# A scratch tile's place, padded gate weights, a float32r mask and moved squares in a hybrid decoder kernel

## The chip, the core and the metric

The kernel runs on one core of one Trainium2 chip. The metric is the device time of one execution in microseconds (us). Engines are named as in the profile: PE is TensorE (matmuls), PEld its weight loads, DVE is VectorE, ACT is ScalarE, POOL is GpSimd, SP is SyncE, which issues the DMAs.

## What is computed

Two layers, one after the other, over 1024 tokens of width 1024 (all float32). A layer normalises its input, projects it, runs four token mixers side by side (stick-breaking attention, a state-space model called S5, retention, a gated linear recurrence called RG-LRU), gates them, and projects back:

```
def _layer(x, ...):
    h = _rms_norm(x, pre_g)
    proj = h @ w_in                                   # 1024 -> 7168
    y_sb  = stick_breaking_attention(q, k, v)         # 4 heads x 64, causal
    y_ssm = s5_branch(ssm_u, ...)                     # 16 groups, 64 complex states
    y_ret = retention(q, k, v)                        # 4 heads x 64
    y_lru = rg_lru_branch(lru_u, ...)                 # 4 blocks x 64, conv of width 4
    mix = stack(y_sb, y_ssm, y_ret, y_lru) * silu(gates)
    y = einsum("bsnw,nwd->bsnd", mix, w_branch)
    out = sum_n(sigmoid(merge_n) * y_n) @ w_out
    return x + _rms_norm(out, post_g)

def rg_lru_branch(u, conv_w, conv_b, w_a, b_a, w_x, b_x, lam):
    xb = conv(u).reshape(..., 4, 64)
    r  = sigmoid(einsum("bsnc,ncd->bsnd", xb, w_a) + b_a)     # gate weights: 64 x 64 blocks
    ig = sigmoid(einsum("bsnc,ncd->bsnd", xb, w_x) + b_x)
    a = exp(-8 * r * softplus(-lam))
    return scan(a, sqrt(1 - a*a) * ig * conv(u))
```

In the attention, a query sees only keys before it: the kernel adds -1e30 to the scores of the others (the causal mask). The S5 branch needs, once per layer, tables that depend on its parameters alone: powers of a complex decay, cosines and sines, products of them with the input and output matrices.

## The kernel before

**Units.** The work is cut into four units: layer 0 and layer 1, each in two chunks of 512 tokens. A unit walks through 64 weight tiles (`filler`): 16 tiles of projections for the mixers, four groups of 10 tiles (gate, merge gate and branch projection, one group for each mixer), and 8 tiles of the output projection. Each float32 product is made of three float32r products of a high and a low part (`mm3`: `hh*wh + hl*wh + hh*wl`), so a weight tile is split first: ACT copies the raw tile to `wh` (L86), DVE subtracts to get `wl` (L89). The splits run a tile and a half ahead of the matmuls; five buffers of `wh` and five of `wl` turn.

**Side tasks.** The mixers and the preparation of the next layer are generators (`first`, `prep`, `lru`, `s5`, `ret`, `sba`, `post`, `prologue`) that are stepped at places between the tiles; the table `PLAN` holds the places. The order of the instructions on each engine is the order in which this Python code issues them; nothing reorders them later. An engine does its instructions in that order, so one that waits holds up all behind it.

**Scratch tiles.** `G()` hands out one of 36 tiles of 128x512 (tag `g`), from a list of free ones. The first instruction that writes a tile waits for the last one that used the same place before.

**The S5 parameter task** (`prep`, L468) runs in unit 0 for layer 0 and in unit 1 for layer 1, nearly all of it on POOL, in some 230 small operations. Its tile `tmp = G()` (L471) is the scratch of the exponentials (`exp_head`, `exp_tail`) and then, as `t1`, of the loop that doubles the cosine and sine tables `tcos` and `tsin` (L432 is the helper `ptt`); the loop's last step, for columns 64 to 127, writes 128x512 in each operation. The DVE operations of `s5` read these tables.

**The gate weights** of RG-LRU (`lru_weights`) are the high part `wlh` (128 rows x 512) and the low part `wll` (256 columns; each block in the 64 rows of its half). In `lru`, for each of two column groups, PE does `wlh`, `wll`, `wlh`, `wll`, where the products with `wll` use 64 rows.

**The mask** (`sba`, for each of 4 token blocks x 4 heads in each unit): two float32r products of queries and keys, padded to at least 256 columns, then a bfloat16 product of the identity `identb` with the 128x128 triangle `trib` into the same bank.

**The first squares** (`first`, the start of unit 0): of eight tiles of the input, POOL squares the first four and sums them (L374, L376), ACT squares the other four, DVE adds those.

Of the kernel before, what the change touches and what calls it, by code (L numbers as in the profile page):

```python
# [9 lines left out]
F32 = mybir.dt.float32  # L10
F32R = mybir.dt.float32r
# [5 lines left out]
P = 128  # L17
# [26 lines left out]
def hybrid_kernel(ctx: ExitStack, tc: tile.TileContext, x, xt, ws1, ws2, par, bcw, preg, postg, con, rot, out, dbg=None):  # L44
# [6 lines left out]
    whp = ctx.enter_context(tc.tile_pool(name="whp", bufs=5))  # L51
    wlp = ctx.enter_context(tc.tile_pool(name="wlp", bufs=5))
    parp = ctx.enter_context(tc.tile_pool(name="parp", bufs=1))
    smp = ctx.enter_context(tc.tile_pool(name="smp", bufs=4))
    genp = ctx.enter_context(tc.tile_pool(name="genp", bufs=NGEN))
    psa = ctx.enter_context(tc.tile_pool(name="psa", bufs=3, space=bass.MemoryType.PSUM))
    psb = ctx.enter_context(tc.tile_pool(name="psb", bufs=5, space=bass.MemoryType.PSUM))
# [65 lines left out]
    xi = v3(cons[:, K_XI:K_XI + 256], P)  # L123
    zeta = cons[:, K_ZETA:K_ZETA + 4]
    cdec = cons[:, K_CD:K_CD + 2]
    identb = const.tile([P, P], BF16, name="identb")
    trib = const.tile([P, P], BF16, name="trib")
    kS = [const.tile([P, SEQ], F32R, name=f"kS{h}") for h in range(4)]
    vsb = const.tile([P, SEQ // P, 256], F32, name="vsb")
    uext = [const.tile([P, 3 + T], F32, name=f"uext{t}") for t in range(2)]  # L130
# [7 lines left out]
    tsin = const.tile([P, 8, P], F32, name="tsin")  # L138
    s5s = const.tile([P, 10, 8], F32, name="s5s")
    RHO, E1C, E1S, HCR, HCI, GCR, GCI = range(7)  # L140
    psc = const.tile([P, 16], F32, name="psc")
    rcar = const.tile([P, 2, 64], F32, name="rcar")
    wgh = const.tile([P, 512], F32R, name="wgh")
    wgl = const.tile([P, 512], F32R, name="wgl")
    wlh = const.tile([P, 512], F32R, name="wlh")
    wll = const.tile([P, 256], F32R, name="wll")
    sp8 = const.tile([P, 2], F32, name="sp8")
    x1 = dram.tile([SEQ, D], F32, name="x1")
    ubuf, ybuf = ([dram.tile([P, T], F32, name=f"{n}buf{h}") for h in range(2)] for n in "uy")
# [193 lines left out]
    def first():  # L343
        pr = S["par", 0] = parp.tile([P, NPAR], F32, tag="par", name=nm("par"))
        gc = pr[:, C_PG:C_PG + 8]
        act.preload_act_table_set(EXPSET)
        xk, xh, xl, sqs = [], [], [], []
        for k in range(KD):
            xk.append(G())
            sp.dma_start(xk[k], xt[k, :, 0:T])  # L350
            if k == 0:
                sp.dma_start(gc, par[0, :, C_PG:C_PG + 8])
                load_to(0)
            if k == 3:
                load_to(1)
        sp.dma_start(pr[:, 0:C_PG], par[0, :, 0:C_PG])
        sp.dma_start(cons[:, 0:P], con[:, 0:P])
        load_to(2)
        load_to(3)
        sp.dma_start(cons[:, P:], con[:, P:])  # L360
        lru_load(0)

        for k in range(KD):
            xh.append(G(F32R))
            xl.append(G(F32R))
            actv(xh[k], xk[k], AF.Identity, scale=gc[:, k:k + 1])
            stt(xl[k], xk[k], gc[:, k:k + 1], xh[k].bitcast(F32), ALU.mult, ALU.subtract)
            if k < 3:
                split_to(k)
            if k == 5:  # L370
                split_to(3)
            if k < 4:
                sqs.append(G())
                pool.tensor_tensor(sqs[k], xk[k], xk[k], op=ALU.mult)  # L374
                if k:
                    pool.tensor_tensor(sqs[0], sqs[0], sqs[k], op=ALU.add)  # L376
        S["h"] = (xh, xl)
        yield 0

        split_to(4)  # L380
        for k in range(4, KD):
            sqs.append(G())
            actv(sqs[k], xk[k], AF.Square)
        for k in range(4, KD):
            tt(sqs[0], sqs[0], sqs[k], ALU.add)
        yield 0
        yield 0
        yield 0
        yield 1
        y = token_rstd(sqs[0])  # L390
        yield 1
        rb = token_rows(y)
        evac_u(rb)
        hh = hp.tile([P, KD, T], F32R, tag="hh", name=nm("hh"))
        hl = hp.tile([P, KD, T], F32R, tag="hl", name=nm("hl"))
        for k in range(0, KD, 2):
            for j in (k, k + 1):
                stt(xk[j], xk[j], gc[:, j:j + 1], rb, ALU.mult, ALU.mult)
                copy(hh[:, j, :], xk[j])
            for j in (k, k + 1):  # L400
                tt(hl[:, j, :], xk[j], hh[:, j, :].bitcast(F32), ALU.subtract)
            yield 0
            if k == 2:
                set_h(hh, hl)
                for t in range(2):
                    dve.memset(uext[t][:, 0:3], 0.0)
                    tt(uext[t][:, 3:3 + T], S.pop(("lps", t)), rb, ALU.mult)
                    S["uext", t] = True
                    Bdone()
        lru_weights()  # L410
# [58 lines left out]
    def prep(l):  # L469
        pr = S["par", l]  # L470
        sc = G()  # L471
        tmp = G()

        def v(i):
            return sc[:, i * 8:(i + 1) * 8]
# [220 lines left out]
    def lru_weights():  # L696

        lw = S.pop("lw")
        w4 = wlh[:, :].rearrange("p (t h c) -> p t h c", t=2, h=2)
        for h in range(2):  # L700
            a, b = slice(64 * h, 64 * h + 64), slice(64 - 64 * h, 128 - 64 * h)
            z = v3(lw[a, 0:256], P)
            copy(w4[a, :, h, :], z)
            copy(w4[b, :, h, :], z)
            tt(v3(wll[a, :], P), z, w4[a, :, h, :].bitcast(F32), ALU.subtract)

    def lru(l, c):
        pr = S["par", l]
# [18 lines left out]
        for t in range(2):  # L727
# [3 lines left out]
            for h in range(2):  # L731
                n = 2 * t + h
                mm(ps[h], wlh[:, n * P:(n + 1) * P], xs[t][h], True, False)
                mm(ps[h], wll[half[h], t * P:(t + 1) * P], xs[t][h][half[h], :], False, True)
            rr[t], ii[t] = G(), G()
            for h in range(2):
                a, b = half[h], half[1 - h]
# [688 lines left out]

    with tc.manual_schedule():
        dve.memset(ones1, 1.0)
        warm = const.tile([P, T], BF16, name="warm")
        dve.memset(warm, 0.0)  # L1430
        ps = A()
        for _ in range(NWARM):
            mm(ps, warm[:, 0:P], warm)
        start("first", first())
        for t in (tmat, ore, oim):
            pool.memset(t, 0.0)
        for u, (l, c) in enumerate(units):
            for i in range(NTILE):
                if u == 0 and i == 8:
# [187 lines left out]
```

## Time and profile before

| | |
|---|---|
| median of 3 runs | 1888.51 us (1888.3 to 1888.53) |
| the profiled execution | 1889.16 us, span of its instructions 1887.4 us |
| mean granted clock of PE | 0.99 |
| busy: PE, DVE, ACT, POOL | 97%, 63%, 47%, 13% of the span |
| DMA | 193.95 MB, 103 GB/s on average |

How to read it: the span is cut by instruction records; "idle before" of an instruction is time in which its engine did nothing, and the name behind it is what ended that. A PE record is longer than the time that a matmul takes of a busy PE, since matmuls are pipelined; from start to start, two matmuls of 512 columns are 0.23 us apart. A granted clock of 1.00 is 2.4 GHz, 0.5 is 1.2 GHz; values between are stretches with both.

### The profile page before, as it was taken

To read this page: it belongs to the slowest core of one execution; us is meant where nothing else is said; L and a number is where in the kernel's file an instruction comes from. 1 tells how busy PE (TensorE), PEld (TensorE's weight loads), DVE (VectorE), ACT (ScalarE), POOL (GpSimd) and SP (SyncE) were. 2 spreads that over 40 slices of the span, in tenths; PEclk is the share of its full clock that TensorE was granted. 3 is DMA by queue.
4 is the path that set the end of the run, shared out by engine and by line. 5 is a ranking of instruction groups with operands and counts; after the bars stand their busy time and mean duration, and the time that the engine had idled before them with its cause. 6 is when DMAs were issued, how large, how long until landed. Compare 5 with 4: busy or idle time off the path is not lost.

```text
span 1887.4 us, 24840 instructions
## 1 busy us (share of the span) xinstructions
PE 1833.0 (97%) x9210; PEld 1501.4 (80%) x9210; DVE 1198.1 (63%) x2165; ACT 884.9 (47%) x1669; POOL 252.0 (13%) x579
## 2 busy tenths in 40 slices
PE   8979999999999999979999999999999999999997
PEld 6757888888878888858888788888888788888886
DVE  7767755455689576635548856655537895776454
ACT  5763444344475444525446634344354845344333
POOL 7872000020000002871200000000000000000001
PEclk9989999999999999989999999999999999999999
DMA  5231232324332222223344223242244322222233
GB/s 175 97 103 60 72 119 91 124 95 151 110 125 98 87 85 68 92 68 134 106 127 145 102 76 109 78 137 95 95 134 133 105 97 87 82 68 79 98 98 106
DMA packets 68856, 193.95 MB, mean 103 GB/s; under 512 B 9600, under 2 KB 18176, under 8 KB 68736
## 3 DMA queue, kind: packets, MB, share of 16 engines
q1 hardware_dynamic: 68736, 192.38, 30.4%
q8 instruction: 72, 1.18, 0.3%
q14 instruction: 48, 0.39, 0.1%
HBM read 179.11 MB, written 12.58 MB: 102 GB/s over the span
## 4 chain that ended last, share of the span: by engine, by line
PE 80%; POOL 8%; DVE 7%; ACT 3%; issue 2%; DMA 1%; SPq 0%; DVEq 0%; ACTq 0%; POOLq 0%
PE pa L101 63%; PE pb L101 15%; POOL g L432 4%; DVE g L89 2%; PE pb L1020 2%; DVE wl L89 1%; ACT g L86 1%; POOL psc L436 1%; DVE g L98 1%; POOL tcos L432 1%; DVE g L93 1%; POOL tsin L432 1%; POOL g L436 1%; ACT g L83 1%; DVE g L811 0%
## 5 line engine op out<-in xcount | busy, mean ns | idle before, releaser
L101 PE MATMUL pa<-hh,wh 128*128 128x512 f32 x1576 | 627.1, 398 | 13.3 <-ACT wh L86 13.3
L101 PE MATMUL pa<-hh,wl 128*128 128x512 f32 x1576 | 617.2, 392 | 17.7 <-DVE wl L89 17.6
L101 PE MATMUL pa<-hl,wh 128*128 128x512 f32 x1576 | 616.0, 391 | 0.0
L89 DVE TENSOR_TENSOR wl<-raw,wh 128x512 fp32r<-128x512 f32 (+1 forms) x512 | 373.5, 767 | 214.8 <-ACT wh L86 214.1
L89 DVE TENSOR_TENSOR g<-g,g 128x512 f32<-128x512 f32 (+7 forms) x432 | 295.8, 685 | 123.9 <-ACT g L86 104.7
L86 ACT ACTIVATE wh<-raw 128x512 fp32r<-128x512 f32 (+1 forms) x512 | 328.2, 686 | 90.0 <-PE pb L101 44.0
L101 PEld LDWEIGHTS pa<-hh,wl 128*128 128x128 f32 x1576 | 297.2, 189 | 83.8 <-DVE wl L89 20.6
L101 PEld LDWEIGHTS pa<-hh,wh 128*128 128x128 f32 x1576 | 297.9, 189 | 75.2 <-ACT wh L86 14.0
L101 PEld LDWEIGHTS pa<-hl,wh 128*128 128x128 f32 x1576 | 297.5, 189 | 58.3 <-DVE hl L89 0.2
L83 ACT ACTIVATE g<-pa 128x512 f32<-128x512 f32 x161 | 96.1, 597 | 497.0 <-PE pa L101 462.2
L89 DVE TENSOR_TENSOR g<-g,pa 128x512 f32<-128x512 f32 x128 | 87.5, 683 | 181.2 <-PE pa L101 164.8
L101 PE MATMUL pa<-g,wh 128*128 128x512 f32 x544 | 169.5, 391 | 4.5 <-DVE g L98 3.4
L86 ACT ACTIVATE g<-pb 128x512 f32<-128x512 f32 (+4 forms) x163 | 72.6, 472 | 143.7 <-PE pb L101 86.0
L906 POOL MEMSET g<- 128x512 f32 x8 | 4.0, 526 | 943.9 <-PE pb L101 943.9
L101 PEld LDWEIGHTS pa<-g,wh 128*128 128x128 f32 x544 | 102.2, 188 | 29.0 <-DVE g L98 5.0
L86 ACT ACTIVATE g<-g 128x512 fp32r<-128x512 f32 (+2 forms) x152 | 79.1, 521 | 71.4 <-DVE g L89 32.8
L101 PE MATMUL pa<-g,wl 128*128 128x512 f32 x272 | 106.0, 390 | 0.0
L83 ACT ACTIVATE g<-pb 128x512 f32<-128x512 f32 (+4 forms) x203 | 87.9, 514 | 23.8 <-PE pb L101 20.1
L86 ACT ACTIVATE g<-pa 64x128 fp32r<-64x128 f32 (+3 forms) x150 | 68.9, 459 | 47.3 <-PE pa L101 45.6
L101 PE MATMUL pa<-wh,g 128*128 128x512 f32 x256 | 79.6, 392 | 0.0
L101 PE MATMUL pb<-wh,g 128*128 128x512 f32 x256 | 79.2, 391 | 0.0
L89 DVE TENSOR_TENSOR g<-pa,g 128x512 f32<-128x512 f32 x51 | 35.7, 702 | 58.9 <-ACT g L83 34.8
(208 smaller groups left out, 2099.6 us busy)
## 6 DMA issues: line engine op xcount, KB each, us to landing
raw<-in_ws_dram SPq DMA_DIRECT2D x128, 640.0 KB, 3.9
raw<-in_ws_dram SPq DMA_DIRECT2D x127, 512.0 KB, 3.6
g<-x SPq DMA_DIRECT2D x32, 256.0 KB, 5.7
g<-in_xt_dram SPq DMA_DIRECT2D x16, 256.0 KB, 6.7
g<-in_x_dram SPq DMA_DIRECT2D x16, 256.0 KB, 3.1
x<-g SPq DMA_DIRECT2D x16, 256.0 KB, 2.1
out_dram<-g SPq DMA_DIRECT2D x16, 256.0 KB, 2.0
g<-in_rot_dram SPq DMA_DIRECT2D x8, 256.0 KB, 4.4
```

Source lines behind the costliest of these rows:

```text
L83: act.activation(out, in_, func, **kw)
L86: act.activation(out, in_, AF.Copy, **kw)
L89: dve.tensor_tensor(out, a, b, op=op)
L93: dve.tensor_scalar(out, a, s1, None, op0=op0)
L98: dve.scalar_tensor_tensor(out, in0=a, scalar=s, in1=b, op0=op0, op1=op1)
L101: pe.matmul(out, lhsT=lhsT, rhs=rhs, start=start, stop=stop)
L432: pool.tensor_tensor(out, a, b, op=op)
L436: pool.tensor_scalar(out, a, s1, None, op0=op0)
L906: pool.memset(t, 0.0)
L1020: pe.transpose(ps[:, q * P:(q + 1) * P], r[:, q * P:(q + 1) * P], ident)
```

## The change

Five edits. `prep` takes its scratch tile from the constant pool (`ptmp`), no longer from the 36 of `G()`. `wll` gets 512 columns and 128 rows like `wlh`, with zeros in the rows of the other half (a POOL memset at the start), and its products use all 128 rows. `identb` and `trib` are float32r. The first four squares go to ACT and their sums to DVE. The warm-up tile comes from `G()`, and the pool of small statistics tiles has three buffers, not four.

```
-    smp = ctx.enter_context(tc.tile_pool(name="smp", bufs=4))
+    smp = ctx.enter_context(tc.tile_pool(name="smp", bufs=3))
...
-    identb = const.tile([P, P], BF16, name="identb")
-    trib = const.tile([P, P], BF16, name="trib")
+    identb = const.tile([P, P], F32R, name="identb")
+    trib = const.tile([P, P], F32R, name="trib")
...
+    ptmp = const.tile([P, 512], F32, name="ptmp")
...
-    wll = const.tile([P, 256], F32R, name="wll")
+    wll = const.tile([P, 512], F32R, name="wll")
...
             if k < 4:
                 sqs.append(G())
-                pool.tensor_tensor(sqs[k], xk[k], xk[k], op=ALU.mult)
-                if k:
-                    pool.tensor_tensor(sqs[0], sqs[0], sqs[k], op=ALU.add)
+                actv(sqs[k], xk[k], AF.Square)
...
-        for k in range(4, KD):
+        for k in range(1, KD):
             tt(sqs[0], sqs[0], sqs[k], ALU.add)
...
     def prep(l):
         pr = S["par", l]
         sc = G()
-        tmp = G()
+        tmp = ptmp
...
-        w4 = wlh[:, :].rearrange("p (t h c) -> p t h c", t=2, h=2)
+        w4, l4 = (w[:, :].rearrange("p (t h c) -> p t h c", t=2, h=2) for w in (wlh, wll))
...
-            tt(v3(wll[a, :], P), z, w4[a, :, h, :].bitcast(F32), ALU.subtract)
+            tt(l4[a, :, h, :], z, w4[a, :, h, :].bitcast(F32), ALU.subtract)
...
                 mm(ps[h], wlh[:, n * P:(n + 1) * P], xs[t][h], True, False)
-                mm(ps[h], wll[half[h], t * P:(t + 1) * P], xs[t][h][half[h], :], False, True)
+                mm(ps[h], wll[:, n * P:(n + 1) * P], xs[t][h], False, True)
...
-        warm = const.tile([P, T], BF16, name="warm")
+        warm = G(BF16)
...
-        for t in (tmat, ore, oim):
-            pool.memset(t, 0.0)
+        for t in (tmat, ore, oim, wll):
+            pool.memset(t if t is not wll else t.bitcast(F32), 0.0)
```

The order of the instructions on PE and DVE stays, apart from those added and removed; what moves are the places of the `g` tiles, and with them the waits. In brackets stand the semaphores that an instruction waits for: `Pool_49` is POOL's count. On DVE in unit 0, at the rotary embedding of retention's keys, stood before (`pa` is a PE bank with a projection, `wl` the low part of a weight half-tile):

```order
L89 TENSOR_TENSOR wl_1198<-raw_1125,wh_1197 128x512 [waits DMAHW1_49,Activation_49]
L89 TENSOR_TENSOR g_1218<-pa_1178,g_1120 128x512 [waits PE_49,Activation_49,Pool_49]
L89 TENSOR_TENSOR g_1217<-g_1217,g_1121 128x512
L89 TENSOR_TENSOR g_1218<-g_1218,g_1217 128x512 [waits DVE_49]
L89 TENSOR_TENSOR wl_1255<-raw_1125,wh_1254 128x512 [waits Activation_49]
L89 TENSOR_TENSOR wl_1271<-raw_1179,wh_1270 128x512 [waits DMAHW2_49,Activation_49]
```

and now, with the same numbers one higher:

```order
L89 TENSOR_TENSOR wl_1199<-raw_1126,wh_1198 128x512 [waits DMAHW1_49,Activation_49]
L89 TENSOR_TENSOR g_1219<-pa_1179,g_1121 128x512 [waits PE_49,Activation_49]
L89 TENSOR_TENSOR g_1218<-g_1218,g_1122 128x512
L89 TENSOR_TENSOR g_1219<-g_1219,g_1218 128x512 [waits DVE_49]
L89 TENSOR_TENSOR wl_1256<-raw_1126,wh_1255 128x512 [waits Activation_49]
L89 TENSOR_TENSOR wl_1272<-raw_1180,wh_1271 128x512 [waits DMAHW2_49,Activation_49]
```

The product into `g_1218` (now `g_1219`) waits for POOL no longer: the count that it waited for was that of POOL's last write to `tsin`, which reads `tmp`, whose place `g_1218` had. On ACT in unit 1, in the second chunk's attention (`pb_7531` holds transposed weights of the attention), stood before:

```order
L83 ACTIVATE g_7527<-pa_7485 128x512 [waits PE_49]
L86 ACTIVATE g_7536<-pb_7531 128x512 [waits PE_49,Pool_49]
L86 ACTIVATE g_7543<-pb_7538 128x512 [waits DVE_49,PE_49]
L86 ACTIVATE wh_7615<-raw_7427 128x640 [waits Activation_49]
L86 ACTIVATE wh_7634<-raw_7486 128x512 [waits DMAHW0_49,DVE_49]
```

and now:

```order
L83 ACTIVATE g_7527<-pa_7485 128x512 [waits PE_49]
L86 ACTIVATE g_7536<-pb_7531 128x512 [waits PE_49]
L86 ACTIVATE g_7543<-pb_7538 128x512 [waits DVE_49,PE_49]
L86 ACTIVATE wh_7615<-raw_7427 128x640 [waits Activation_49]
L86 ACTIVATE wh_7634<-raw_7486 128x512 [waits DMAHW0_49,DVE_49]
```

The same wait for POOL's last `tsin` is gone there. New waits for POOL stand where DVE's part of S5 in unit 0 first reads the tables:

```order
L1057 SCALAR_TENSOR_TENSOR g_1510<-g_1510,ones_119 128x127
L89 TENSOR_TENSOR g_1511<-g_1511,g_1510 128x127 [waits DVE_49,PE_49]
L89 TENSOR_TENSOR g_1562<-pb_1552,tcos 128x512 [waits PE_49,Pool_49]
L89 TENSOR_TENSOR g_1564<-pb_1553,tsin 128x512 [waits PE_49,Pool_49]
L89 TENSOR_TENSOR g_1562<-g_1562,g_1564 128x512 [waits DVE_49]
```

Before, these two had no wait of their own for POOL, since DVE had waited for the same count earlier.

## Rows read from the trace of the kernel before

**Rows 1.** The page, engines: busy us, share of the span, instructions.

```profile
PE 1833.0 (97%) x9210; PEld 1501.4 (80%) x9210; DVE 1198.1 (63%) x2165; ACT 884.9 (47%) x1669; POOL 252.0 (13%) x579
```

**Rows 2.** The chain that ended last: start us, us, what (count).

```profile
248.44 13.68 PE pa L101 x60
```

**Rows 3.** Waits of PE, the longest: waiter, releaser, total us, times, longest.

```profile
PE pa L101 <- DVE wl L89: 17.8, 6, 10.4
PE pa L101 <- ACT wh L86: 13.8, 2, 13.3
```

**Rows 4.** Timeline of PE in unit 0: start us, us, instruction, idle before.

```profile
109.12 0.40 PE L101 MATMUL pa<-hl,wh 128*128 128x512 f32 x1
119.97 0.79 PE L101 MATMUL pa<-hh,wl 128*128 128x512 f32 x1 [10.44 <-DVE wl L89]
...
124.37 0.27 PE L1020 MATMUL pb<-cons,g 128*128 128x128 f32 x1
```

**Rows 5.** Timeline of DVE in unit 0.

```profile
98.17 1.48 DVE L89 TENSOR_TENSOR wl<-raw,wh 128x512 fp32r<-128x512 f32 x2
117.26 0.69 DVE L89 TENSOR_TENSOR g<-pa,g 128x512 f32<-128x512 f32 x1 [17.60 <-POOL tsin L432]
...
144.42 0.68 DVE L89 TENSOR_TENSOR g<-pb,tcos 128x512 f32<-128x512 f32 x1
```

**Rows 6.** Timeline of POOL, the last write of the table in units 0 and 1.

```profile
115.96 1.26 POOL L432 TENSOR_TENSOR tsin<-tsin,g 128x512 f32<-128x512 f32 x1
...
837.51 1.26 POOL L432 TENSOR_TENSOR tsin<-tsin,g 128x512 f32<-128x512 f32 x1
```

**Rows 7.** Stretches: length, busy us (count) of PE, PEld, DVE, ACT, POOL, clock, DMA.

```profile
120.00:124.40 4.40, 4.40 (x11) 3.35 (x12) 4.26 (x8) 0.00 (x0) 0.00 (x0) 0.51 0.68 209
...
840.50:844.60 4.10, 4.04 (x10) 3.01 (x11) 3.92 (x6) 2.05 (x5) 0.00 (x0) 0.51 0.52 155
```

**Rows 8.** Timeline of PE in unit 1.

```profile
826.84 0.39 PE L101 MATMUL pa<-hh,wl 128*128 128x512 f32 x1
840.56 0.79 PE L101 MATMUL pa<-hh,wh 128*128 128x512 f32 x1 [13.34 <-ACT wh L86]
...
844.57 0.63 PE L101 MATMUL pa<-g,wh 128*128 128x512 f32 x2
```

**Rows 9.** Timeline of ACT in unit 1.

```profile
838.80 1.08 ACT L86 ACTIVATE g<-pb 128x512 f32<-128x512 f32 x2 [23.40 <-POOL tsin L432]
```

**Rows 10.** Timeline of PE at RG-LRU's gates, unit 0, first of eight such places.

```profile
61.65 0.40 PE L101 MATMUL pb<-g,wlh 128*128 128x512 f32 x1
61.98 0.50 PE L101 MATMUL pb<-g,wll 64*128 64x512 f32 x1
...
63.60 0.40 PE L101 MATMUL pb<-hl,wh 128*128 128x512 f32 x1
```

**Rows 11.** Timeline of PE at a mask, unit 0, one of 64.

```profile
200.24 0.23 PE L101 MATMUL pb<-trib,identb 128*128 128x128 bf16 x1
...
200.59 0.40 PE L101 MATMUL pa<-hl,wh 128*128 128x512 f32 x1
```

**Rows 12.** Timeline of PE at plain float32 products of 128 columns.

```profile
231.37 0.39 PE L101 MATMUL pb<-g,ore 128*128 128x128 f32 x2
231.60 0.39 PE L101 MATMUL pb<-g,oim 128*128 128x128 f32 x2
```

**Rows 13.** Timeline of DVE, ACT and PE at the start.

```profile
5.82 0.69 DVE L89 TENSOR_TENSOR wl<-raw,wh 128x512 fp32r<-128x512 f32 x1 [0.41 <-ACT wh L86]
...
12.02 1.77 DVE L89 TENSOR_TENSOR wl<-raw,wh 128x512 fp32r<-128x512 f32 x1
13.72 3.89 DVE L98 SCALAR_TENSOR_TENSOR g<-g,par,g 128x512 fp32r<-128x512 f32 x3
...
15.33 2.18 ACT L83 ACTIVATE g<-g 128x512 f32<-128x512 f32 x4
...
15.29 0.50 PE L101 MATMUL pa<-g,wh 128*128 128x512 f32 x1 [1.48 <-DVE g L98]
```

## The prediction

> **What bounds the kernel now.** I read the page's engine shares first: PE is busy 97% of the span and POOL 13% [rows 1]. So a gain must come out of PE's time, and a slow engine matters only where PE waits for it. The chain of waits gives the price of a normal matmul: 60 of 512 columns in 13.68 us, 0.228 us each [rows 2]; this is the unit for everything below. Then PE's waits: the two lines that lead them, 17.8 and 13.8 us, hold one wait of 10.4 us behind DVE and one of 13.3 behind ACT [rows 3]. Both were followed back on the timelines.
>
> In unit 0, PE goes from a matmul at 109.12 straight to the next at 119.97 [rows 4]. It waits for a `wl`; DVE, which makes it, sat idle for 17.60 us until POOL's last `tsin` [rows 5], which ended at 115.96 + 1.26 = 117.22 [rows 6]. The instruction that DVE stood at is a rotary product that has nothing to do with the tables: by the order it writes a `g` tile on the place that `tmp` had, and `tmp` is read by that last `tsin`. In unit 1 the same happens on ACT: a copy of attention weights waits 23.40 us for `tsin` [rows 9], which ends at 838.77 [rows 6], the weight splits queue behind the copy, and PE stands from 826.84 to 840.56 [rows 8]. After each stop PE runs at a granted clock of 0.51, that is mostly 1.2 GHz, over the next 4 us [rows 7]. It had been idle just before both times.
>
> **The change part by part.** All against the profiled execution's 1889.16 us.
>
> 1. *The scratch tile.* The two waits for POOL are gone from the order, at the row that stalled in each case. First stop: 119.97 - 109.12 = 10.85 us where 0.23 is normal, so 10.62; then ten matmuls in 124.37 - 119.97 = 4.40 us where 2.28 is normal, so 2.12 for the low clock [rows 4]. Together 12.7. Second stop: 840.56 - 826.84 - 0.23 = 13.49, then nine matmuls in 844.57 - 840.56 = 4.01 against 2.05, so 1.96 [rows 8]. Together 15.4. Sum 28.2 (before rounding) us, all on PE's path. What is late next? DVE gets its idle 17.60 us back and then leads PE by more than before, since PE's own stop was shorter by 7 us. The tables are first needed at 144.42, by DVE [rows 5]; with 13 to 15 us taken away before it, that read comes at about 130, and POOL is done at 117.22 even if it gains nothing. So the new wait for POOL there finds its count reached.
>
> 2. *Full-row `wll`.* From the first `wlh` at 61.65 to the second ordinary matmul after the group at 63.60 there are five intervals, 1.95 us where five normal ones are 1.14 [rows 10]. The 0.81 us is lost wherever 64-row and 128-row products follow each other. There are eight such places (4 units x 2 column groups, 16 products with `wll`): 6.5 us. With 128 rows the form is that of any other float32r product, so I take all of it; the other end is nothing. The memset of `wll` and the strided write of its halves lie on POOL and DVE with nobody waiting. The Trainium skill, "TensorE: Matmul & The Clock Gate", section "Why this matters for your kernels", speaks against this edit: a product with few rows takes the time of a full one, and its gain is that it can run beside others. By that rule padding buys nothing and this term is 0, so the sum would be 6.5 us smaller. The row disagrees here, with 0.39 us for an interval where the rule has 0.23, so I go by the row.
>
> 3. *The float32r mask.* Before, from the mask to the second matmul behind it is 200.59 - 200.24 = 0.35 us: mask plus one full product [rows 11]. No float32r product under 256 columns is in the trace, so the price is bounded by the float32 ones of 128 columns: two records in 0.23 us, 0.115 each [rows 12]. If float32r does it in one such pass, the group takes 0.115 + 0.228 = 0.343: 64 masks gain 0.5 us. If it needs two, as each plain float32 product does, it takes 0.23 + 0.228, 0.108 more than now: 64 masks lose 6.9. I take one pass, since all wider float32r products run as one record each.
>
> 4. *The first squares.* POOL's squares run beside DVE and both slow: the same `wl` takes 0.69 us alone and 1.77 beside a square, and three of the low parts of the input take 3.89, 1.30 each; PE stops for the fourth at 15.29 [rows 13]. Without POOL's squares DVE wins 1.08 + 0.61 = 1.7 there and more before it, while the squares that ACT now does (0.55 each, four in 2.18 us) stand partly before the high parts. I take a gain of 1.5 us. Ends: the two waits of this kind, 3.0 gained, and all four squares on the path, 2.2 lost. The three extra adds on DVE, 0.7 each, come in its queue before the fifth and later weight splits; they lie beside matmuls of the first tiles, and if they did not, they would be 2 us.
>
> 5. *The rest at nothing.* POOL starts the S5 task some us earlier, which after edit 1 nobody waits for; if that cover were gone, it would be a gain. The warm-up tile in `G()` is free long before its place is taken again. The small tiles that lose a buffer are written and read by DVE in its own order in the attention, so a third buffer is enough.
>
> Sum: 28.2 + 6.5 + 0.5 + 1.5 = 36.7. 1889.16 - 36.7 = 1852.5; the profiled execution lies 0.65 above the median of the runs, so 1851.8 for a median.
>
> **The rivals.** *The mask needs two passes*: 7.4 us worse than assumed, 1859.2. For it: the code pads the query products to 256 columns, as if fewer were dear. Against: the wider ones show no sign of a second pass. 18%.
>
> *Half rows are not the cause* of the 0.81 us at the gates (the change of operands could be): 1858.3. This is what the page's rule above would make of it. Against: the neighbours with 128 rows follow each other at 0.23, with changing operands. 4%.
>
> *One of the two stops only moves*: another `g` tile lands on a place that POOL, or an engine behind it, holds long, or DVE's queue is too full in the stretch that is now denser. That gives back 12.7 or 15.4: 1864.5 or 1867.2. For it: DVE is close to full after the first stop, 4.26 of 4.40 us [rows 7]. Against: the order shows POOL's count at no other instruction near the two. 11%.
>
> *The change does not free the place*: the tile is freed, but the first writer there waits for POOL by another tile. That is 28.2 back, 1880.0. Against: the order's rows. 1%.
>
> *Slower than before.* Only the mask is repeated often enough: 64 times on PE. It would have to eat the other 36.2 us, 0.57 us more for each mask than now, over twice a full 512-column product, for instance if its weights could not be loaded beside the product before. The mixed forms at the gates cost 0.16 more for a product (0.39 against 0.23) [rows 10]. It decides from 0.57 us on: at 0.63, 64 x 0.63 = 40.3 against 36.2, 1892.6. 3%.
>
> **How the numbers follow.** 63% for the forecast's own case. The forecast is 1851.8. The range: below, squares at their better end and some us of small waits at the start and in unit 0, 1846; above, the mask's two passes (1859.2) with the squares at their worse end (3.7 more), or the first stop moved (1864.5), 1865. About 0.2%, 3.8 us, can be told from no change by measurement. Every case but the last is faster by more than that: the nearest to 1888.5 is the place that is not freed, 8.5 us below. So faster 0.95, slower 0.03, and 0.02 for within 0.2%, taken off the faster cases (a mask somewhat dearer than two passes, or errors that add up).
>
> **What would show it.** In the profile after: no wait of DVE or ACT for `tsin` over 1 us, no gap of PE over 6 us, and granted clock 1.00 where the two stops were; `wll` with 128 rows and 0.23 us from start to start; the mask as 64 records (128 would be two passes), with some 0.34 us to the second matmul behind it; the first `wl` splits at 0.7 us and PE's tile 1 done 1 to 2 us earlier. Wrong would be: PE's stops back at other places under another name, a mask that takes over 0.4 us, or POOL's tables still on the chain.

## The result, and the profile after

The changed kernel takes 1861.72 us (median of 4 runs, 1861.34 to 1862.88), the kernel before 1888.52 (4 runs, 1888.3 to 1888.82). The ratio is 0.986 with a 95% interval of 0.9842 to 0.9876: 26.8 us faster where 36.7 were forecast. The time lies in the stated range, but a quarter of the gain is missing. The profiled execution took 1862.88 us, its span is 1861.1.

The page's engine line, to be laid beside [rows 1]:

```profile
PE 1826.2 (98%) x9210; PEld 1508.6 (81%) x9210; DVE 1200.8 (65%) x2168; ACT 888.2 (48%) x1673; POOL 258.1 (14%) x573
```

PE is still the bound, and its busy time shrank by 6.8 us (1833.0 to 1826.2): 19.5 of the 26.3 us by which the span is shorter are waiting that went. Its longest waits are no longer those of [rows 3]:

```profile
PE pa L101 <- DVE wl L89: 13.5, 8, 4.2
...
PE pa L101 <- ACT wh L86: 0.5, 1, 0.5
```

Of the 13.8 us behind ACT 0.5 are left. Behind DVE the longest is now 4.2 (a stop in unit 2 that was 4.69 before), but there are eight waits where there were six. Two of the new ones stand in unit 0, where the first stop was [rows 4]:

```profile
111.18 0.27 PE L1019 MATMUL pb<-cons,g 128*128 128x128 f32 x1
...
117.91 0.50 PE L101 MATMUL pa<-hh,wl 128*128 128x512 f32 x1 [2.91 <-DVE wl L89]
...
126.04 0.50 PE L101 MATMUL pa<-hh,wl 128*128 128x512 f32 x1 [2.39 <-DVE wl L89]
```

The row at 111.18 is the one that stood at 124.37: PE reaches it 13.2 us earlier, as forecast. Then it stands twice, for a low part each time. The reader should now look at DVE in that stretch, against [rows 5]:

```profile
108.05 1.30 DVE L89 TENSOR_TENSOR wl<-raw,wh 128x512 fp32r<-128x512 f32 x2 [4.54 <-ACT wh L86]
...
113.44 0.69 DVE L89 TENSOR_TENSOR g<-pa,g 128x512 f32<-128x512 f32 x1
114.05 2.36 DVE L89 TENSOR_TENSOR g<-g,g 128x512 f32<-128x512 f32 x2
116.33 2.98 DVE L89 TENSOR_TENSOR wl<-raw,wh 128x512 fp32r<-128x512 f32 x2
119.23 0.68 DVE L89 TENSOR_TENSOR g<-pa,g 128x512 f32<-128x512 f32 x1
...
124.49 2.43 DVE L89 TENSOR_TENSOR wl<-raw,wh 128x512 fp32r<-128x512 f32 x2
```

and at POOL beside it, against [rows 6]:

```profile
110.80 1.45 POOL L431 TENSOR_TENSOR tcos<-tcos,g 128x512 f32<-128x512 f32 x1
112.21 1.95 POOL L431 TENSOR_TENSOR ptmp<-tsin,g 128x512 f32<-128x512 f32 x1
...
118.84 1.63 POOL L431 TENSOR_TENSOR tsin<-tsin,ptmp 128x512 f32<-128x512 f32 x1
```

No wait for `tsin` is left. But POOL's last table step, which before ran from 110.50 while DVE stood still for it, now runs beside DVE's work, and both are slower: POOL's six operations take 1.45 to 1.95 us where they had 1.04 to 1.26, and two low parts take 2.98 us at 116.33 against 1.30 at 108.05.

One wait of DVE for POOL is left in this stretch, and it stood there before too, outside the rows of the prediction. First the kernel before, then the changed one:

```profile
148.58 0.69 DVE L89 TENSOR_TENSOR g<-pb,tcos 128x512 f32<-128x512 f32 x1 [1.33 <-POOL g L432]
```

```profile
142.24 0.69 DVE L89 TENSOR_TENSOR g<-pb,tcos 128x512 f32<-128x512 f32 x1 [1.67 <-POOL g L431]
```

It is not for the tables. In the program of either kernel this product writes a `g` tile on the place that `sc` had, the other scratch tile of `prep` (one line above `tmp`), and waits for the last POOL product that reads `sc`. It is the same kind of wait as the one that edit 1 takes away; experiment 4 comes back to it.

How much PE is ahead of the kernel before, at the same matmul of both traces:

| matmul (start before, after) | ahead | what lies between |
|---|---|---|
| 22.36, 19.88 | 2.47 | the opening |
| 29.91, 29.16 | 0.75 | low clock in after |
| 80.09, 77.77 | 2.32 | gates of unit 0, two places |
| 94.16, 93.41 | 0.75 | two waits for low parts |
| 124.37, 111.18 | 13.19 | the first stop is gone |
| 136.88, 130.70 | 6.18 | the two new stops |
| 175.95, 171.32 | 4.63 | low clock behind a stop of 1.85 |
| 826.84, 820.32 | 6.51 | gates of unit 1, masks |
| 844.57, 822.59 | 21.98 | the second stop is gone |
| 1799.95, 1773.67 | 26.28 | gates of units 2 and 3, the stop in unit 2, masks |

The places of low clock, by stretches (columns as in [rows 7]; the clock is the last but two):

```profile
24.00:28.00 4.00, 4.00 (x12) 3.30 (x12) 3.33 (x16) 0.00 (x0) 3.06 (x12) 0.59 0.79 259
...
127.00:131.00 4.00, 4.00 (x16) 2.59 (x16) 3.93 (x7) 1.63 (x4) 3.92 (x7) 0.57 0.85 311
168.00:172.00 4.00, 4.00 (x19) 3.71 (x18) 1.52 (x3) 2.12 (x4) 0.84 (x2) 0.57 0.00 0
```

In each of them PE is busy throughout, much of the time at the lower level of 1.2 GHz. None of the three stretches was low in the kernel before.

The other edits, first the gates (columns as in [rows 10]):

```profile
60.94 0.39 PE L101 MATMUL pb<-g,wlh 128*128 128x512 f32 x1
61.17 0.39 PE L101 MATMUL pb<-g,wll 128*128 128x512 f32 x1
61.40 0.39 PE L101 MATMUL pb<-g,wlh 128*128 128x512 f32 x1
61.63 0.40 PE L101 MATMUL pb<-g,wll 128*128 128x512 f32 x1
61.87 0.39 PE L101 MATMUL pb<-hh,wh 128*128 128x512 f32 x1
```

0.23 us from start to start, as wanted. Then a mask, against [rows 11]:

```profile
195.72 0.22 PE L101 MATMUL pb<-trib,identb 128*128 128x128 f32 x1
195.78 0.44 PE L101 MATMUL pa<-hh,wh 128*128 128x512 f32 x1
196.06 0.40 PE L101 MATMUL pa<-hl,wh 128*128 128x512 f32 x1
```

One record for each mask and 0.34 to the second matmul behind it: one pass.

### The profile page after: what moved, and what is told of

Same layout as the page of the kernel before. It is cut to its first block, busy times and chain, and to the rows that moved or that the text cites. A ratio compares the mean times of both kernels' runs of the same rounds, so it can differ in the third digit from the quotient of the medians.

```text
span 1861.1 us, 24840 instructions
## 1 busy us (share of the span) xinstructions
PE 1826.2 (98%) x9210; PEld 1508.6 (81%) x9210; DVE 1200.8 (65%) x2168; ACT 888.2 (48%) x1673; POOL 258.1 (14%) x573
## 4 chain that ended last, share of the span: by engine, by line
PE 85%; DVE 8%; ACT 5%; issue 1%; DMA 1%; SPq 0%; DVEq 0%; ACTq 0%
PE pa L101 66%; PE pb L101 16%; DVE g L89 2%; PE pb L1019 2%; ACT g L86 2%; ACT g L83 1%; DVE wl L89 1%; DVE g L98 1%; DVE g L93 1%; ACT wh L86 1%; DMA raw<-in_ws_dram 1%; DVE g L810 0%; PE pb L254 0%; ACT kS L86 0%; DVE g L1057 0%
## 5 line engine op out<-in xcount | busy, mean ns | idle before, releaser
L83 ACT ACTIVATE g<-g 128x512 f32<-128x512 f32 (+2 forms) x98 | 57.1, 602 | 31.1 <-DVE g L89 22.8
```

Of the source, the lines that this page charges most:

```text
L83: act.activation(out, in_, func, **kw)
```

## The experiments

Twelve runs follow; the ratios are against the kernel before, measured beside them (medians 1888.07, 1889.25 and 1887.95). Times of four executions of one kernel spread over 1 us and more, so beside the times one measure of the trace is used throughout: how long PE takes from the last matmul before the first stop (109.12 in before) to a matmul behind the stretch (170.52 in before). It is 61.40 us in before, and would be 61.40 - 12.7 = 48.7 with the first stop taken out. In after it is 164.32 - 108.40 = 55.92. The missing 7.2 us are what most of the experiments are about.

**1. The scratch tile alone** (`b_ptmp`, on the kernel before):

```
+    ptmp = const.tile([P, 512], F32, name="ptmp")
...
-        tmp = G()
+        tmp = ptmp
```

> The kernel before with edit 1 alone: the scratch tile has its own place. Theory A (after the first stop DVE is the bound of its stretch, and its late work meets POOL's last table step): of the first stop only some 5 to 6 us stay won at PE, the second stop is won whole (15.5), so 1888.5 - 21 = 1867.5, within 1.5, with PE standing again for 2 to 3 us each at the next two low parts of the weights. Rival B (the sum of the prediction: both stops lie whole on PE's path): 1888.5 - 28.2 = 1860.3, and what the changed kernel lacks against 1851.8 comes from another edit.

Measured: 1869.13 us (1866.45 to 1871.75), ratio 0.9897 (0.988 to 0.9913). PE's measure is 56.66, nearly that of after. In the trace the second stop gives back 15.5, the first 6.65 at first, of which 2.06 go by 151 (1.5 of it at a stop that experiment 4 explains) and 3.10 by 174, the latter mostly at low clock. So rival B falls: the edit by itself does not bring 28.2, and what is missing does not come from another edit. Theory A is right on the second stop and too kind on the first: 1.5 stay there by 174, where it had 5 to 6. The new stop:

```profile
118.82 0.80 PE L101 MATMUL pa<-hh,wl 128*128 128x512 f32 x1 [3.14 <-DVE wl L89]
```

**2. The full-row gate weights alone** (`b_wll`, on the kernel before): the wider `wll`, its memset, and

```
-                mm(ps[h], wll[half[h], t * P:(t + 1) * P], xs[t][h][half[h], :], False, True)
+                mm(ps[h], wll[:, n * P:(n + 1) * P], xs[t][h], False, True)
```

> The kernel before with edit 2 alone: full-row gate weights. Theory A (in this kernel the first stop ends at a time that POOL sets, so what PE wins before it in unit 0 is waited away): six of the eight places count, 6 x 0.81 = 4.9, so 1883.6. Rival B (all eight count): 6.5, so 1882.0. By the page's rule that few rows take the time of a full product and padding wins nothing: 1888.5.

Measured: 1885.99 us (1885.18 to 1888.13, 10 runs), ratio 0.999 (0.998 to 0.9999). In the trace each of the eight places gives its 0.80, 6.4 in all, so the edit does what the row promised. By the rule of the Trainium skill that the prediction names nothing would be won; the trace does not bear that out. But only 3.3 reach the end. In unit 0 PE is 1.55 ahead at 85.95, 0.62 at 87.10 and no longer at 94.21; the rest went in two stretches where the low clock lasted longer (0.65 behind the second stop, 1.01 in unit 2). Where the 1.6 go, PE shows:

```profile
87.10 0.50 PE L101 MATMUL pa<-hh,wl 128*128 128x512 f32 x1 [0.77 <-DVE wl L89]
94.21 0.51 PE L101 MATMUL pa<-hh,wl 128*128 128x512 f32 x1 [1.38 <-DVE wl L89]
```

and DVE, with the low parts in question:

```profile
86.36 1.30 DVE L89 TENSOR_TENSOR wl<-raw,wh 128x512 fp32r<-128x512 f32 x2
...
93.36 1.45 DVE L89 TENSOR_TENSOR wl<-raw,wh 128x512 fp32r<-128x512 f32 x2
```

In the kernel before the same low parts start at 86.41 and 93.42, 0.05 later: DVE did not move, though PE came 1.6 earlier. Theory A had the loss in the right unit and at the wrong place: not the first stop swallows it, but these two short waits ahead of it.

**3. The last table step left out** (`a_nolast`, on the changed kernel). It leaves out the last doubling of layer 0's cosine and sine tables, columns 64 to 127, and fills them with constants:

```
+            if l == 0 and j == 6:
+                pool.memset(tcos[:, :, hi], 1.0)
+                pool.memset(tsin[:, :, hi], 0.0)
+            else:
                 ptt(tcos[:, :, hi], tcos[:, :, lo], cb, ALU.mult)
...
```

> The changed kernel, but in layer 0 the last step of the table's doubling (six POOL operations of 128x512) is left out and two POOL memsets fill the columns. Theory A1 (PE's two new stops, 2.91 and 2.39 us, come from DVE being slowed by POOL's table step beside it): DVE's low parts near 116 go from 1.49 to about 0.65 each, the first stop falls to about 0.8 us, the second to nothing, and the low clock after it goes: 1861.7 - 4.5 to 6 = 1856 to 1857. Rival A2 (DVE has simply too much in its queue there, POOL or not): the stops stay within 1 us of 2.91 and 2.39, and the time within 1.5 of 1861.7.

Measured: 1858.52 us (1855.37 to 1859.92), ratio 0.9842 (0.9827 to 0.9857). PE's measure falls from 55.92 to 51.78. The stops:

```profile
115.29 0.50 PE L101 MATMUL pa<-hh,wl 128*128 128x512 f32 x1 [0.91 <-DVE wl L89]
...
122.48 0.50 PE L101 MATMUL pa<-hh,wl 128*128 128x512 f32 x1 [1.46 <-DVE wl L89]
```

2.4 us in place of 5.3, and no low clock between 100 and 160. The first stop came out as A1 said; the second stayed at 1.46 where A1 had nothing. That does not show a queue of DVE that is too full without POOL, for POOL is at work there too:

```profile
117.68 1.82 DVE L98 SCALAR_TENSOR_TENSOR g<-g,g 128x512 f32<-128x512 f32 x1
117.65 1.31 POOL L431 TENSOR_TENSOR wgl<-g,wgh 128x512 fp32r<-128x512 f32 x1 [3.52 <-ACT wgh L86]
```

The same DVE operation takes 0.69 in after, at 121.67, so 1.13 of the 1.46 may be this one meeting. Of the missing 7.2 us the table step is 4.1.

**4. The table step done twice** (`a_twice`, on the changed kernel), the opposite of 3:

```
+            for _ in range(2 if l == 0 and j == 6 else 1):
+                ptt(tcos[:, :, hi], tcos[:, :, lo], cb, ALU.mult)
...
```

> The changed kernel with the last step of layer 0's table doubling done twice (the same six POOL operations of 128x512 again, with the same result). Theory A1 (POOL's wide operations slow DVE beside them): the second round runs from 120 to about 130, DVE's operations there take half as long again or more, and PE's second stop grows from 2.39 to 4 or more. Rival A2: the stops near 115 and 124 stay within 0.7 of 2.91 and 2.39. Under both, DVE's wait for POOL near 142 grows from 1.67 to 8 to 11, so the whole time is 1867 to 1873 either way; the stops decide, not the time.

Measured: 1868.59 us (1867.3 to 1871.45), ratio 0.9895 (0.988 to 0.991). PE's measure rises to 60.83, by 4.9. The stops:

```profile
120.77 0.79 PE L101 MATMUL pa<-hh,wl 128*128 128x512 f32 x1 [5.42 <-DVE wl L89]
...
130.56 0.50 PE L101 MATMUL pa<-hh,wl 128*128 128x512 f32 x1 [2.38 <-DVE wl L89]
```

It was the first stop that grew, not the second, and DVE's later wait for POOL grew only to 3.03, not to 8 or more; both expectations were off there. The amount speaks plainly: a table step less takes 4.1 us off PE's time in this stretch, one more puts 4.9 on. In DVE's own time, from the start of the two low parts at 108.05 to the end of those at 124.49, the same 22 operations without a gap in each trace:

| | us |
|---|---|
| before (119.23 to 134.48; POOL idle for 10.86 of it) | 15.25 |
| `a_nolast` (107.07 to 123.37) | 16.30 |
| after (108.05 to 126.92) | 18.87 |
| `a_twice` (108.37 to 131.25) | 22.88 |

Both runs change a second thing, the end of POOL's work, and with it the wait for the place of `sc`: DVE's product with `tcos` that waits there starts at 136.91 in `a_nolast` and at 142.24 in after. Here are it and PE's stop that follows, in `a_twice`:

```profile
148.12 0.69 DVE L89 TENSOR_TENSOR g<-pb,tcos 128x512 f32<-128x512 f32 x1 [3.03 <-POOL g L431]
154.87 1.15 PE L101 MATMUL pb<-g,g 128*64 128x64 f32 x32 [0.64 <-DVE g L89]
```

In six traces (`a_twice`, `b_ptmp`, `a_bf16`, `a_poolsq`, `a_half2`, `after_again`) PE stands at this matmul, for 0.64 to 1.45 us, and each time starts it 6.75 or 6.76 us after that DVE product, and ends the measure 21.43 to 21.45 after it. There POOL's last use of `sc` sets the end, by way of DVE. In after PE comes to this matmul by itself, 7.41 after the DVE product, only 0.66 later than this would have let it. So two things hold PE back, the late low parts and the place of `sc`, and they nearly tie. Up to a matmul ahead of this wait (136.88 in before) the table step alone shows: 18.20 us in `a_nolast`, 22.30 in after, 26.53 in `a_twice`, 27.75 in before. But with the two stops gone and POOL's work as it ran in after, PE would, by these numbers, have waited for some 6.6 of the 7.2 us at the later place. This is an estimate: no run moves `sc`.

**5. The order of DVE's work** (`a_lru2`, on the changed kernel): the two scans of RG-LRU behind the low parts that PE waits for.

```
-        "lru": (12, 13, 14, 15, 17, 21, 28, 29),
+        "lru": (12, 13, 14, 15, 17, 21, 30, 31, 33),
...
-("lru", GATE0)
+("lru", GATE0 + (u == 0))
```

> The changed kernel, but in unit 0 the last three steps of RG-LRU (exponentials, two scans) are taken one to two half-tiles later, so that DVE makes the low parts of the next weights before the scans. Theory A2 (the low parts are late because the scans stand before them in DVE's queue): both stops fall under 0.5 us, 1861.7 - 5.3 = 1856.4, with the low clock behind the second gone too 1855. Rival A1 (DVE has no time to spare while POOL works beside it, in whatever order): the stops come back within the next two tiles, and the time is within 1.5 of 1861.7.

Measured: 1863.46 us (1862.53 to 1864.6), ratio 0.9871 (0.9856 to 0.9885). PE's measure is 56.94, 1.0 more than in after. The stops:

```profile
122.16 0.50 PE L101 MATMUL pa<-hh,wl 128*128 128x512 f32 x1 [3.04 <-DVE wl L89]
136.03 0.51 PE L101 MATMUL pa<-g,wh 128*128 128x512 f32 x1 [0.61 <-DVE g L89]
143.38 0.63 PE L897 MATMUL pb<-cons,g 128*128 128x128 f32 x4 [0.95 <-DVE g L89]
149.30 1.15 PE L101 MATMUL pb<-g,g 128*64 128x64 f32 x32 [1.43 <-DVE g L89]
```

The stop at 117.91 is gone, and its time comes back at four others: A2 falls, and the time lies 0.3 outside A1's range. In this order too DVE has no time to spare there; the order only chose where PE stands.

**6. The table step earlier** (`a_par2`, on the changed kernel): the parameters are loaded with the first tile, and five steps of `prep` stand one half-tile earlier.

```
-                sp.dma_start(gc, par[0, :, C_PG:C_PG + 8])
+                sp.dma_start(pr, par[0])
...
-        "prep": (2, 3, 4, 6, 7, 10,
+        "prep": (1, 2, 3, 5, 6, 10,
```

> The changed kernel, but layer 0's parameters are loaded with the first tile and the S5 parameter task's first steps stand one to two half-tiles earlier, so that POOL is through with the last table step 7 to 9 us earlier (by about 112, not 120.4). Theory A1 (the stops come from POOL's table step beside DVE's full stretch from 108 on): the step falls mostly where DVE is idle, the two stops fall from 5.3 us to under 2.5 in all, 1858 to 1859.5. Rival A2 (DVE has too much there in any case): both stops stay, 1861.7 within 1.

Measured: 1863.63 us (1862.06 to 1864.89), ratio 0.9859 (0.9843 to 0.9876): no gain. PE's measure does fall, to 53.37, with three stops of 4.0 in all: 2.5 won, less than hoped, as the step still ends at 114.8 and DVE's full stretch begins at 110.4. And 4.25 are lost before, between 38 and 51, since ACT's tanh and sine, with two table loads of 1.28, now come ahead of the weights' high parts; 1.5 of it is low clock behind the wait at 46.01:

```profile
46.01 0.50 PE L101 MATMUL pa<-wh,hh 128*128 128x512 f32 x1 [1.60 <-ACT wh L86]
```

**7. The mask in bfloat16** (`a_bf16`, on the changed kernel): `identb` and `trib` as before.

> The changed kernel with identity and triangle of the mask in bfloat16 again. If float32r goes in one pass: each of the 64 masks takes 0.01 to 0.02 us more in bfloat16, 0.6 to 1.3 in all, 1862.3 to 1863. If float32r needs two: 64 x 0.11 less, 1854.7. Seen in the trace as the time from a mask to the second product behind it.

Measured: 1863.58 us (1862.82 to 1867.05), ratio 0.9865 (0.985 to 0.988). The times alone can't tell 0.8 us; the traces can. The median time from a mask to the second matmul behind it is 0.356 in bfloat16 (0.355 in before) and 0.343 in after: 0.012 to 0.013 for each mask, 0.8 us for 64. One pass.

**8. The squares on POOL** (`a_poolsq`, on the changed kernel): edit 4 undone.

> The changed kernel with the first four squares and their sums on POOL again. Theory C (PE's gain at the start, 2.5 us, is waited away by 94, since ACT and DVE hand each other work there and set the pace): the start is 2 to 2.5 us slower and the rest of unit 0 takes it back; the time stays at 1861.7 within 1, and the low clock behind 25 is gone. Rival D (the prediction's term holds to the end): 1863.2. POOL's tables begin about 2 us later here, which under A1 costs up to 1 more.

Measured: 1863.74 us (1863.35 to 1864.61), ratio 0.9863 (0.9849 to 0.9878). The trace goes against C: PE is 1.8 us behind after's at 77, and still 1.9 at 108; the waits at 86 and 94 are as long as in after, only later. So what is won or lost at the start lasts (as it seems, because the chain of ACT and DVE behind it starts from there; no run shows that), while what is won at the gates does not (experiment 2). How much it is stays uncertain. In this trace the low clock falls in the opening, which puts it 1.1 behind even the kernel before; in six traces with the edit and an unchanged `PLAN` PE is 0.40 (`a_twice`), 0.56 (`a_bf16`), 0.72 (after), 1.54 (`after_again`), 1.69 (`a_nolast`) and 2.08 (`a_half2`) ahead of before at 108.

**9. Half rows in another order** (`a_half_hhll`, on the changed kernel), 64 rows for the low part again, but both high products first:

```
+            for h in range(2):
+                n = 2 * t + h
+                mm(ps[h], wll[half[h], n * P:(n + 1) * P], xs[t][h][half[h], :], False, True)
```

> The changed kernel with the products of the low part of the gate weights on 64 rows again, and in another order: both products with the high part, then both with the low part, so that at each of the eight places 64-row and 128-row products follow each other twice and not four times. Theory M (each change between the two forms costs, 0.81 over four changes = 0.2 each): 0.4 lost at each place in the trace, 3.2 in all, 1861.7 + 3.2 = 1865. Rival N (each 64-row product costs its own 0.4): 0.81 at each place, 6.5, 1868. By the page's rule (few rows take the time of a full product, no more): nothing lost, 1861.7.

Measured: 1865.63 us (three executions, 1864.88 to 1865.98). The fourth, the profiled one, took 6487 us with all its work stretched, so there is no usable trace and the kernel ran again (`a_half2`).

> The half-row products in the order high, high, low, low once more, for a usable trace of the eight places. Theory M (0.2 for each change between 64 and 128 rows): 0.4 lost at each place, 3.2 in all against the changed kernel in this call. Rival N (0.4 for each 64-row product): 0.81 at each place, 6.5. By the page's rule: nothing.

Measured: 1863.08 us (1861.71 to 1864.02), ratio 0.9863 (0.9848 to 0.9878), beside 1862.17 for the changed kernel (experiment 10). PE at the first place:

```profile
59.83 0.40 PE L101 MATMUL pb<-g,wlh 128*128 128x512 f32 x1
60.16 0.50 PE L101 MATMUL pb<-g,wll 64*128 64x512 f32 x2
60.59 0.50 PE L101 MATMUL pb<-hh,wh 128*128 128x512 f32 x1
60.92 0.39 PE L101 MATMUL pb<-hl,wh 128*128 128x512 f32 x1
```

The two half-row products start 4 ns apart and take 0.50 us together: they run side by side, each in its half of the rows. From the first high product on, five intervals are 1.32 us here, 1.15 in after, 1.95 in before, the same at seven of the eight places. The two changes of form still cost 0.33 - 0.23 ahead of the pair, 0.43 - 0.23 behind it and 0.33 - 0.23 one later, 0.4 together, which is M's price; but the pair saves one product of 0.23, so 0.17 is lost at a place, 1.4 in all. M had the cost of a change right and missed the saving; N, with 0.81 at a place, falls. One more reading fits these two orders: 0.4 for each 64-row product, with the two costs of a pair side by side. The kernel before has a row that speaks against it, in retention, where eight plain float32 products on 64 rows follow each other, two records of 128 columns each:

```profile
160.24 0.39 PE L101 MATMUL pa<-hh,wl 128*128 128x512 f32 x1
160.56 1.16 PE L101 MATMUL pb<-g,g 64*128 64x128 f32 x16
...
161.99 0.39 PE L101 MATMUL pa<-hl,wh 128*128 128x512 f32 x1
```

From 160.24 to 161.99 are 1.75 us. Two full products at 0.228 and eight pairs at 0.115, the price of one record of [rows 12], make 1.38. So 0.37 is lost for all sixteen records, the price of two changes of form. The Trainium skill, "TensorE: Matmul & The Clock Gate", section "Why this matters for your kernels", says both that a product with few rows takes the time of a full one and that such products gain by running at the same time in different row groups; the second half is what this trace shows. The first half leaves out the changes between the forms, and they are all that edit 2 wins.

**10. The changed kernel again** (`after_again`).

> The changed kernel once more, beside the other three on the same chip. All theories: 1861 to 1863, with PE's two stops of 2 to 3 us near 115 and 124 again. It tells two things besides: how far a session moves the times, and whether the stretches of low clock (near 25, 127 and 168 in the first profile) come at the same places. If they are a matter of chance, at least one of the three is missing or moved.

Measured: 1862.17 us (1861.14 to 1862.74), ratio 0.9858 (0.9842 to 0.9875). PE's measure is 55.86, but in other portions: one stop of 3.44 near 114, a longer low clock behind it, and one of 0.83 at 148.77 (the place of `sc`, experiment 4); the low clock at 25 is missing, that at 168 is there. So the places of low clock are in part a matter of chance. The stop of 1.8 us near 165 shows it best, since it stands in all thirteen traces. In after the 24 small products behind it take 4.00 us:

```profile
166.56 4.00 PE L101 MATMUL pb<-g,g 128*128 128x128 f32 x24 [1.85 <-DVE g L89]
```

and in `a_bf16`, after the same wait and in the same order:

```profile
166.97 2.89 PE L101 MATMUL pb<-g,g 128*128 128x128 f32 x24 [1.84 <-DVE g L89]
```

Eight traces have low clock behind this stop (3.60 to 5.06 us for the 24 products), five (before among them) have none. Thirty matmuls behind the stop it has cost 1.6 to 3.3 us.

**11. Three places moved** (`a_best`, on the changed kernel): the parameters' load as in 6, `prep` from (2, 3, 4, 6, 7, 10, ...) to (1, 2, 3, 6, 7, 10, ...), and in unit 2

```
-        "lru": (6, 8, 10, 12, 13, 14, 17, 21, 24, 25),
+        "lru": (6, 8, 10, 12, 13, 14, 17, 26, 28),
```

> The changed kernel with three places moved: layer 0's parameters are loaded with the first tile, the first three steps of the S5 parameter task stand one half-tile earlier (its tables end some 4 us earlier), and in unit 2 the two scans of RG-LRU come two to three half-tiles later. Theory A1 with DVE's queue as the cause in unit 2: the two stops of unit 0 fall from 5.3 to about 4 in all, the stop of 4.23 in unit 2 falls under 2 and its low clock goes: 1857, within 1.5. Rival A2 (DVE has no time to spare in either place): 1861 to 1863.

Measured: 1859.91 us (1859.44 to 1860.86), ratio 0.9848 (0.9833 to 0.9862). All its times lie below all those of the changed kernel in experiment 10, 2.3 us at the median: it is the fastest kernel here that computes everything. The gain is that of unit 2, where after's stop of 4.23 becomes two:

```profile
1031.14 0.50 PE L101 MATMUL pa<-hh,wl 128*128 128x512 f32 x1 [1.88 <-DVE wl L89]
1038.31 0.50 PE L101 MATMUL pa<-hh,wl 128*128 128x512 f32 x1 [1.43 <-DVE wl L89]
```

and the low clock behind it is gone. In unit 0 A1 as I put it fails: the table step, from 106.16 on and so 4.6 us earlier, now lies over the first operations of DVE's full stretch, and PE's measure is 57.46, worse than in after. Earlier by 4 us was no cure, and a step that is over before 107 wasn't tried.

## Why the prediction was right, and where it was wrong

**The second stop (15.4).** Right: 21.98 - 6.51 = 15.47 in the trace. There POOL's last table step runs beside a DVE that has little to do (2.04 us busy of 7 between 829 and 836), and nothing is late next.

**The first stop (12.7).** The stop itself went as forecast: 13.19 - 0.72 = 12.47 by 111.18. The step that failed is the answer to "What is late next?": "DVE gets its idle 17.60 us back and then leads PE by more than before", with POOL "done at 117.22 even if it gains nothing". The 17.60 us were not free time. In them POOL did its widest operations alone; with the wait gone they fall on DVE's fullest stretch, the same 22 DVE operations take 18.87 in place of 15.25, and PE waits for the low parts: 7.0 given back by 130.70, and 1.6 more at low clock behind the stop near 165 (which is chance, experiment 10). Experiments 3 and 4 show it by taking the step away and by doubling it, and in 5 another order of the queue brings nothing. 3.9 of the 12.7 stayed.

The same answer asked of POOL only when the tables are done. Item 5 put the rest of POOL's S5 task at nothing ("which after edit 1 nobody waits for"), but in the kernel before DVE waited 1.33 us for it at 148.58, by the place of `sc`, 4 us behind the row that the prediction looked at. In six traces this wait sets the end of the stretch (experiment 4), and of the 3.1 us that `a_nolast` still lacks to 48.7 it would, by the same 6.75, hold back 2.2 in any case. So the slowing of DVE is shown to make the two stops; how much of the 8.6 it costs by itself, with `sc` out of the way, stays open.

The evidence lay in the prediction's own step 4: [rows 13] show POOL's squares making a low part 1.77 in place of 0.69. It was used for the squares and not for the tables. The rule is on a page, too: the Trainium skill, "SBUF — State Buffer", section "Who interferes with whom", says that a VectorE instruction with two inputs in SBUF contends with a GpSimd instruction that reads SBUF, and that one with at most one such input, outside its two-port modes, does not. The trace agrees: `g<-pa,g`, with one input from a PE bank, takes 0.69 and 0.68 in the middle of the table step, as ever, while `wl<-raw,wh` goes from 0.65 to 1.49; and beside `a_nolast`'s memsets, which read nothing, DVE's `g<-g,g` at 110.47 takes 0.73.

**The rival "one of the two stops only moves"** had the right place and, in "DVE's queue is too full in the stretch that is now denser", half the cause. It had 12.7 given back and 11%; 8.6 were. It deserved more, for [rows 7] show DVE busy 4.26 of 4.40 us behind the first stop.

**The gates (6.5).** The price was right, 0.80 at each of eight places. The 1.6 of unit 0 were taken as PE's alone, and PE is not the bound of what comes before 94: with PE 1.6 earlier DVE's low parts come 0.05 earlier (experiment 2). 4.8 reach the end. A share of 97% for the whole span told nothing of this stretch.

**The mask (0.5).** One pass, as taken; 0.012 to 0.013 a mask, 0.8 in all, not 0.5. The two rivals that rest on it fall (1859.2, and the slower one).

**The squares (1.5).** DVE's low parts take 0.69 in the opening, as forecast, and PE is 2.47 ahead at 19.88; the low clock takes 1.7 of it in the profiled execution. By 108 between 0.40 and 2.08 are left (experiment 8), in after 0.72: the forecast of 1.5 lies within, and with a spread so wide that is in part luck.

**The rest.** 0.7 came in unit 2 around its stop, uncounted. The sum by the trace: 15.5 + 3.9 + 4.8 + 0.8 + 0.7 + 0.7 = 26.4, against 26.28 at the last matmul of the table.

**The rival "half rows are not the cause"** falls by the 0.80 at every place in experiment 2, and experiment 9 names the cause more exactly: the change of form.

**The total.** The first stop brought 8.8 us less than its term, the gates 1.7 and the squares 0.8; the mask and unit 2 gave 1.0 back. That the time lies within the range is in part luck: its upper end was set by the mask's two passes, which did not come, and by the whole first stop given back, of which two thirds were.

## What to carry to other kernels

When a wait is taken away, ask what the engine waited for was doing meanwhile: if the two then run side by side and share something, part of the wait comes back as slower work. Price the freed stretch with both engines' operations at their slowed durations, which the trace often shows elsewhere. When one scratch tile proves to hold a place too long, look at its neighbours too: here `sc` was left where `tmp` was moved. And ask of every small gain on the bounding engine whether it bounds in that very stretch: follow the next wait behind the gain to its engine, and see whether that engine would move too.

## What the runs showed of the hardware that was not expected

- A product on 64 rows among products on 128 costs nothing extra by its own size: each change between the two forms costs about 0.2 us (0.37 for sixteen 64-row records in a row, with two changes), and two 64-row products on different halves of the rows, issued one after the other, start 4 ns apart and take 0.50 us together.
- POOL beside DVE costs both: POOL's 128x512 operations take 1.45 to 1.95 us in place of 1.04 to 1.26, DVE's with both inputs in SBUF about twice their time (1.49 in place of 0.65), DVE's with an input from a PE bank no more than ever (0.69).
- After one and the same stop of 1.8 us PE's granted clock fell in eight traces and did not in five, with 3.60 to 5.06 or 2.89 us for the 24 products behind it: a term of a few us can't be judged by one profiled execution.
